# A two-layer hybrid decoder trunk: work at the chunks' ends moved by a few ticks, and the last pair of one mixer turned on TensorE

## The chip, the cores and the metric

The kernel runs on one core of a Trainium2 chip. The metric is the device time of one execution in microseconds (us), the median of the runs. All data is float32; every product of the projections is made of three matmuls of float32r parts.

## The reference

Two layers over 256 tokens of width 2048. Each layer is one RMS norm, one input projection, two mixers, a gate, and an output projection that is added to the residual stream; a last norm closes.

```python
def layer_even(x, norm_g, w_in, w_out):
    h = rmsnorm(x, norm_g)
    qa, ka, va, iq, ik, iw, qb, kb, vb, gate = split_cols(h @ w_in, SPLIT0)
    ...                      # rotary embedding on qa, ka, iq, ik, qb, kb
    o_a = dsa_attention(qa, ka, va, iq, ik, iw)   # 10 heads, one shared key/value head, 64 keys chosen per query
    o_b = dilated_attention(qb, kb, vb)           # 6 heads, three dilated windows, merged
    y = concatenate([o_a, o_b], axis=-1)
    return x + (y * silu(gate)) @ w_out

def layer_odd(x, norm_g, w_in, b_f, w_out):
    h = rmsnorm(x, norm_g)
    qc, kc, vc, qd, kd, vd, fl, gate = split_cols(h @ w_in, SPLIT1)
    o_c = stick_breaking_attention(qc, kc, vc)    # 8 heads; reverse cumulative sums of log(1 - sigmoid(z))
    log_f = log_sigmoid(fl + b_f)
    o_d = forgetting_attention(qd, kd, vd, log_f) # 8 heads; softmax with a running sum of log_f
    y = concatenate([o_c, o_d], axis=-1)
    return x + (y * silu(gate)) @ w_out
```

Each mixer's head makes scores of its queries and keys (causal), weights of the scores, and the weights times its values.

## The kernel before, in words

**Projections.** The columns of the two input and the two output projections are cut into 39 chunks ("jobs") of up to 512 columns, and TensorE does the jobs one after another; they are numbered from 0 (B5 is job 13, P0 job 14). Layer 0 has the jobs B0, K, I0, I1, B1, B2, B3, A0, A2, A4, A6, A8, B4, B5: a B job holds q, k, v and gate of one head, an A job q and gate of a pair of heads (A8 is the last pair, the heads 8 and 9), K and I are keys and indexer. P0 to P3 are the output projection. Layer 1 has C0, F1, G1, C2 to C7, D0 to D7, then Q0 to Q3. A job has 16 k-tiles of 128 input rows. For each k-tile and each half of the tokens, `products` (L323, L324, L326) issues hi times x-hi, hi times x-lo and lo times x-hi: six matmuls. One k-tile is a "tick".

**Weights.** SyncE loads them in pieces of four k-tiles, 1 MB (`load`, L256, tile raw, three buffers). For each half of a piece, `split` makes whi on ScalarE (L282, a rounding copy) and wlo on VectorE (L283, the rest). There are four buffers of each, so the splitting runs three halves ahead of TensorE. The first pieces are smaller, and x^T (tile xst) comes between them: `load_xT` (L626) sends the third and fourth k-tile from ScalarE's queue, the others from SyncE's.

**The work round of a head.** What a head needs beside its projection is written as a generator: it issues instructions, and `yield n` lets n ticks pass. After each k-tile `tick` advances all running generators, so their instructions land in each engine's queue between those of the splitting. Each engine, SyncE with its DMAs among them, works through its queue in the order in which it was issued. The round of a chunk begins when its projection ends, and runs beside the next two or three jobs on TensorE.

**Turning.** Queries, keys, weights of the attention and gates must be transposed. The "far" way is a 32x32 block transpose on VectorE into the tile far (`grid`, L428), a write to DRAM (`moved`, L437, tile fard) and a read-back (L448, or L442 where four reads keep the blocks in order). `gate_turned` does this for a gate at once, `gate_late` eight ticks later (L511). The "near" way is a transpose on TensorE (`turn`, L400, tile tp) and a cut from PSUM. Before, only B4, B5, D6 and D7 use it for their weights, and B5 and D7 for queries, keys and gate as well.

**The heads.** `heads_a` does a pair of A heads: rotary, gate u (L769), far turn of qk, scores and softmax of each head (`soft`, L549 and L551), weights (`share`, L565) turned far, cut into pAh/pAl and pBh/pBl (L477, L478), and six products into o (L464 to L466). For C and D, `vg1` makes v and the gate u by way of e = exp, a reciprocal on VectorE (L882) and two multiplications (L887); `stick` is the C head's weights (Exp, Ln and Relu on ScalarE, L939 to L942, a scan on VectorE, L945), `softmax_head` the D head's. The output products of all heads share one PSUM bank, o, and are multiplied by the turned gate uT (L532, L809).

Of the kernel before, what the change touches and what calls it, by code (L numbers as in the profile page):

```python
# [14 lines left out]
P = 128  # L15
# [159 lines left out]
def trunk(ctx, tc, x, xT, g1, w0, wo0, w1, wo1, bf, gf, consts, rope, out):  # L175
# [66 lines left out]
    def load():  # L242
        i = st["load"]
        if i == len(pieces):
            return
        st["load"] += 1
        wd, off, n, w = pieces[i]
        if i < len(FIRST):

            kt = sum(FIRST[:i])  # L250
            raws[i] = home[kt // 8][:, (kt % 8) * w:(kt % 8 + n) * w]
        else:
            raws[i] = wp.tile([P, n * w], F32, name="raw", tag="raw")
        if i == 1 or 3 < i < len(FIRST):
            load_xT(kt)
        nc.sync.dma_start(raws[i], wd[off:off + P * n * w].rearrange("(p f) -> p f", p=P))  # L256
        if i in (0, 2):
            load_xT(i)
        if i == len(FIRST) + 1:
            for th in range(NT):  # L260
                for c0, c1 in ((0, D),):
                    nc.sync.dma_start(xs[:, th, c0:c1], x[th * P:(th + 1) * P, c0:c1])
            nc.sync.dma_start(rt.rearrange("p a b -> p (a b)"), rope)
        if i == len(FIRST) + 2:
            nc.sync.dma_start(cons, consts)
# [235 lines left out]

    def gate_late(u, n=NT):

        box = []

        def way():
            yield 8
            t = grid([u])
            d = dr.tile([P, P * n], F32, name="fard", tag=f"fard{n}", bufs=4)
            yield 2  # L510
            nc.sync.dma_start(d, t)  # L511
            yield 4
            uT = hp.tile([P, P * n], F32, name="uT", tag="uT" if n == NT else "rl")
            read_back(uT, d, n)
            box.append(arrived(uT, n))

        start(way())
        return box
# [59 lines left out]

    def softmax_head(qk, ticks, nb, v, u, rs, kt, last, near):

        uT = u if last else gate_turned(u)
        qk = yield from qk_turned(qk, ticks, last)
        pr, l = soft(qk, nb() if callable(nb) else nb)
        if not last:
            yield 2
        share(pr, factor(l, rs))
        if near:
            yield 4
            blocks = quarters(turn([pr[:, 0:P], pr[:, P:SEQ], pr[:, SEQ:384]]))
        else:  # L590
            yield from moved(grid([pr]), pr, 2, 4, True)
            yield 4
            blocks = arrived(pr, 3)
        yield from weights_out(blocks, v, uT, kt, last)
# [14 lines left out]
    def load_xT(kt):  # L609
# [11 lines left out]
        for k in range(kt, kt + n):  # L621
            if k == kt or k == 9:
                m = min(kt + n, 9 if k < 9 else KT) - k
                t, j = (xst["a"], k - 1) if k < 9 else (xst["b"], k - 9)
                q = nc.scalar if k == 2 else nc.sync
                q.dma_start(t[:, j:j + m, :].rearrange("p a b -> p (a b)"), xT[:, KT + k * SEQ:KT + (k + m) * SEQ])  # L626

# [132 lines left out]
    def heads_a(ps, h):  # L760
# [3 lines left out]
        for th in range(NT):  # L764
            rotate(qk[:, th * 256:(th + 1) * 256], ps[th][:, 0:256], rt[:, th, 0:P], rt[:, th, 256:384], 2, P)
            tgs[1 - th] = hp.tile([P, 256], F32, name="tg", tag="tg")
            nc.scalar.activation(tgs[1 - th], ps[1 - th][:, 256:512], AF.Tanh, scale=hr0[:, 1 - th:2 - th])
        for th in (1, 0):
            nc.vector.scalar_tensor_tensor(u[:, :, th, :], tgs[th].rearrange("p (a b) -> p a b", a=2), 1.0,  # L769
                                           ps[th][:, 256:512].rearrange("p (a b) -> p a b", a=2),  # L770
                                           op0=OP.add, op1=OP.mult)
        uT = gate_late(u.rearrange("p a b c -> p (a b c)"), 4)
        yield from far([qk], qk, 2, 2, 4)
        yield 4
        q = arrived(qk, 4)
# [7 lines left out]
        js = [slice(j * P, (j + 1) * P) for j in range(2)]  # L783
        away = []
        for j in range(2):
            pr, l = soft((f[:, js[j]], kA, hi[:, js[j]], lo[:, js[j]], kAh, kAl), nbA)
            yield 2
            share(pr, factor(l, hr0))

            t = hp.tile([P, 512], F32, name="far", tag=("ih2", "il2")[j], bufs=1)[:, 0:384]  # L790
            start(moved(grid([pr], t), t, 2, 4, True))
            away.append(arrived(t, 3))
            yield 2
        yield 4

        ph, pl = (hp.tile([P, 2, SEQ], F32R, name="pA" + n, tag="i" + n, bufs=1) for n in "hl")
        p1h, p1l = (hp.tile([P, 2 * P], F32R, name="pB" + n, tag=t, bufs=1) for n, t in (("h", "y"), ("l", "sp")))
        for j in range(2):
            cut((quarters(ph[:, j, :]), quarters(pl[:, j, :])), away[j][:, 0:2])
            cut((quarters(p1h[:, js[j]]), quarters(p1l[:, js[j]])), away[j][:, 2:3])  # L800
            yield (8, 3)[j]
        uT, = uT
# [66 lines left out]

    def vg1(ps, o, apart=False, third=False):  # L870

# [3 lines left out]
        for th in range(NT):  # L875
            t = slice(th * P, (th + 1) * P)
            nc.scalar.activation(e[:, t], ps[th][:, o + P:o + 256], AF.Exp, scale=nr1[:, th:th + 1])  # L877
            upper(th)
        if apart:
            yield 1  # L880
        nc.vector.tensor_scalar(e, e, 1.0, 3.0e38, op0=OP.add, op1=OP.min)
        nc.vector.reciprocal(e, e)  # L882
        if apart:
            yield 1
        for th in range(NT):
            t = slice(th * P, (th + 1) * P)
            nc.vector.scalar_tensor_tensor(u[:, t], ps[th][:, o + P:o + 256], r1[:, th:th + 1], e[:, t],  # L887
                                           op0=OP.mult, op1=OP.mult)
        lower()
        return v, u  # L890
# [39 lines left out]
    def stick(qk, ticks, v, u, kt):  # L930

        uT = gate_late(u)
        qk = yield from qk_turned(qk, ticks, 0)
# [5 lines left out]
        nc.scalar.activation(sp, z, AF.Abs)  # L939
        nc.scalar.activation(sp, sp, AF.Exp, scale=-1.0)  # L940
        nc.scalar.activation(sp, sp, AF.Ln, bias=1.0)
        nc.scalar.activation(zp, z, AF.Relu)  # L942
        yield 6
        for _, s in BLK:
# [5 lines left out]
        yield from moved(grid([z]), z, 2, 4, True)  # L950
        yield 10
        yield from weights_out(arrived(z, 3), v, uT, kt, 0, 5)

    def head_c(ps, h):
        qk = scaled_qk(ps, 0, (0, 3), (1, 2))
        start(moved(grid([qk]), qk, 2, 4))
        v, u = yield from vg1(ps, 256, h == 0, h % 3 == 2)
        yield from stick(qk, 10 if h else 8, v, u, h)

    def head_cf(ps, qk):  # L960
        v, u = yield from vg1(ps, 0)
        yield from stick(qk, 10, v, u, 1)

    def head_d(ps, h):
        qk = scaled_qk(ps, 1, (0, 3), (1, 2))
        last = 2 * (h == HDD - 1)
        if not last:
            start(moved(grid([qk]), qk, 2, 4))
        v, u = yield from vg1(ps, 256, third=h == 0)
        yield from softmax_head(qk, 10, lambda: biases[h], v, u, None, HC + h, last, h >= HDD - 2)  # L970

# [125 lines left out]
```

## Time and profile before

| | |
|---|---|
| median of 3 runs | 898.07 us (895.04 to 900.7) |
| profiled execution | 896.82 us |
| its span, first to last instruction | 894.7 us |
| TensorE busy / its weight loads | 879.1 us (98%) / 734.5 us |
| VectorE, ScalarE, GpSimd busy | 659.0, 475.3, 50.2 us |
| DMA | 207.59 MB, 232 GB/s in the mean |
| chain that ended last | PE 79%, DVE 8%, DMA 6%, issue 3%, ACT 3% |

Matmuls overlap in the array: a row of the timeline gives start and duration, and the pace is read from one start to the next. A bracket such as [0.88 <-DVE wlo L283] is time for which the engine stood idle before this row, and what ended it. PE is TensorE, DVE VectorE, ACT ScalarE, SP SyncE, SPq its queue of DMA issues.

### The profile page before, as it was taken

The numbers are of one execution on the slowest core, as the hardware profiler recorded it, in microseconds if no ns is written. First come the engines' busy times: TensorE is split into PE (matmuls) and PEld (weight loads), VectorE is DVE, ScalarE is ACT, GpSimd is POOL, SyncE is SP. The second block draws the span as 40 slices with busy tenths as digits, with TensorE's granted clock in tenths as the row PEclk, the third lists the DMA queues.
The fourth block names the chain that finished last, engine by engine and source line by source line (L and its number), as shares of the span: only waits on it lengthen the run. The fifth ranks groups of instructions, "written<-read, shape, count | busy, mean of one in ns | idle before, by whom it ended". The sixth has DMA issues, their size and how long they took to land.

```text
span 894.7 us, 12055 instructions
## 1 busy us (share of the span) xinstructions
PE 879.1 (98%) x4185; PEld 734.5 (82%) x4185; DVE 659.0 (74%) x1162; ACT 475.3 (53%) x840; POOL 50.2 (6%) x69
## 2 busy tenths in 40 slices
PE   9999999999999999999999999999999999999996
PEld 6988888888888877888898888888777888888886
DVE  7587888877777777666667777777787777776563
ACT  7644555454454555555455555555555555555440
POOL 0013100000000000000000000000010000001110
PEclk9999999999999999999999999999999999999998
DMA  9887555676777765766486756666685776665542
GB/s 360 316 314 268 209 204 192 209 265 208 258 247 234 228 219 210 277 229 243 146 287 222 254 202 238 217 231 224 231 281 202 268 236 244 236 219 182 192 185 95
DMA packets 89661, 207.59 MB, mean 232 GB/s; under 512 B 32112, under 2 KB 60800, under 8 KB 71424
## 3 DMA queue, kind: packets, MB, share of 16 engines
q1 hardware_dynamic: 88128, 203.52, 64.7%
q0 software_dynamic: 896, 2.12, 0.8%
q10 hardware_dynamic: 576, 1.19, 0.4%
q8 instruction: 33, 0.54, 0.2%
q14 instruction: 28, 0.23, 0.1%
HBM read 185.29 MB, written 21.50 MB: 231 GB/s over the span
## 4 chain that ended last, share of the span: by engine, by line
PE 79%; DVE 8%; DMA 6%; issue 3%; ACT 3%; SPq 1%; POOL 0%; DVEq 0%; POOLq 0%; ACTq 0%
PE pj L323 25%; PE pj L324 25%; PE pj L326 25%; DVE wlo L283 3%; DMA raw<-in_w_out_dram 2%; DMA qk<-fard 2%; ACT whi L282 2%; DMA raw<-in_w_in_dram 1%; DMA fard<-far 1%; DVE far L428 1%; DVE e L882 1%; PE s L538 1%; PE o L531 0%; PE s L465 0%; PE s L466 0%
## 5 line engine op out<-in xcount | busy, mean ns | idle before, releaser
L283 DVE TENSOR_TENSOR wlo<-raw,whi 128x1024 fp32r<-128x1024 f32 (+3 forms) x300 | 352.6, 1189 | 149.7 <-ACT whi L282 148.2
L323 PE MATMUL pj<-whi,xh 128*128 128x512 f32 (+3 forms) x992 | 378.5, 383 | 0.0
L324 PE MATMUL pj<-whi,xl 128*128 128x512 f32 (+3 forms) x992 | 376.4, 381 | 0.0
L282 ACT ACTIVATE whi<-raw 128x1024 fp32r<-128x1024 f32 (+3 forms) x300 | 299.8, 1025 | 123.6 <-PE pj L324 73.4
L326 PE MATMUL pj<-wlo,xh 128*128 128x512 f32 (+3 forms) x992 | 297.3, 381 | 1.9 <-DVE wlo L283 1.8
L326 PEld LDWEIGHTS pj<-wlo,xh 128*128 128x128 f32 x992 | 182.9, 188 | 39.8 <-DVE wlo L283 4.5
L323 PEld LDWEIGHTS pj<-whi,xh 128*128 128x128 f32 x992 | 186.7, 188 | 34.0 <-ACT whi L282 1.3
L324 PEld LDWEIGHTS pj<-whi,xl 128*128 128x128 f32 x992 | 186.6, 188 | 33.0
L323 PE MATMUL pj<-whi,yh 128*128 128x512 f32 (+1 forms) x248 | 95.7, 386 | 0.0
L324 PE MATMUL pj<-whi,yl 128*128 128x512 f32 (+1 forms) x248 | 94.9, 383 | 0.0
L326 PE MATMUL pj<-wlo,yh 128*128 128x512 f32 (+1 forms) x248 | 76.7, 382 | 0.0
L326 PEld LDWEIGHTS pj<-wlo,yh 128*128 128x128 f32 x248 | 46.6, 188 | 9.2
L324 PEld LDWEIGHTS pj<-whi,yl 128*128 128x128 f32 x248 | 46.7, 188 | 8.7
L323 PEld LDWEIGHTS pj<-whi,yh 128*128 128x128 f32 x248 | 46.6, 188 | 8.6
L477 ACT ACTIVATE yh<-uT 128x256 fp32r<-128x256 f32 (+1 forms) x27 | 12.4, 458 | 61.1 <-DVE uT L532 45.2
L551 ACT ACTIVATE sn<-sn,nm 128x128 f32<-128x128 f32 (+1 forms) x48 | 21.5, 449 | 35.2 <-DVE nm L549 35.2
L598 ACT ACTIVATE sq<-xs 128x512 f32<-128x512 f32 x23 | 14.3, 623 | 30.2 <-DVE xs L821 26.5
L882 DVE RECIPROCAL e<-e 128x256 f32<-128x256 f32 x16 | 28.1, 1753 | 0.6
L382 POOL TENSOR_TENSOR qk<-rot,rot 128x256 f32<-128x256 f32 x16 | 11.9, 741 | 230.3 <-ACT sn L551 109.7
L948 ACT ACTIVATE z<-z 128x384 f32<-128x384 f32 x8 | 4.2, 526 | 38.0 <-DVE z L947 38.0
L877 ACT ACTIVATE e<-pj,nr 128x128 f32<-128x128 f32 x32 | 11.8, 367 | 21.9 <-DVE qk L867 21.9
L478 DVE TENSOR_TENSOR yl<-uT,yh 128x256 fp32r<-128x256 f32 (+1 forms) x27 | 12.8, 475 | 14.3 <-ACT yh L477 14.3
(216 smaller groups left out, 715.0 us busy)
## 6 DMA issues: line engine op xcount, KB each, us to landing
raw<-in_w_in_dram SPq DMA_DIRECT2D x108, 1024.0 KB, 6.1
raw<-in_w_out_dram SPq DMA_DIRECT2D x32, 1024.0 KB, 4.9
fard<-far SPq DMA_DIRECT2D x43, 256.0 KB, 2.1
qk<-fard SPq DMA_DIRECT2D x25, 256.0 KB, 5.2
fard<-far SPq DMA_DIRECT2D x28, 192.0 KB, 2.0
raw<-in_w_in_dram SPq DMA_DIRECT2D x4, 672.0 KB, 10.0
fard<-far SPq DMA_DIRECT2D x20, 128.0 KB, 4.6
uT<-fard SPq DMA_DIRECT2D x20, 128.0 KB, 4.2
```

Of the source, the lines that this page charges most:

```text
L282: nc.scalar.activation(hi, rw, AF.Copy)
L283: nc.vector.tensor_tensor(lo, rw, hi.bitcast(F32), op=OP.subtract)
L323: nc.tensor.matmul(o, a, wh, start=(kt == 0), stop=False)
L324: nc.tensor.matmul(o, b, wh, start=False, stop=False)
L326: nc.tensor.matmul(o, a, wl, start=False, stop=(kt == KT - 1))
L382: nc.gpsimd.tensor_tensor(dst, t1[:, 0:n], t2[:, 0:n], op=OP.add)
L477: nc.scalar.activation(dst[0], src, AF.Copy)
L478: nc.vector.tensor_tensor(dst[1], src, dst[0].bitcast(F32), op=OP.subtract)
L551: nc.scalar.activation(sn[:, s], sn[:, s], AF.Exp, scale=-1.0, bias=nm[:, th:th + 1], accum_out=l[:, th:th + 1])
L598: nc.scalar.activation(j, xs[:, th, c * 512:(c + 1) * 512], AF.Square, accum_out=ss[:, i, th, c:c + 1])
L877: nc.scalar.activation(e[:, t], ps[th][:, o + P:o + 256], AF.Exp, scale=nr1[:, th:th + 1])
L882: nc.vector.reciprocal(e, e)
```

## The change

It moves instructions of the work round by a few ticks and, for one pair of heads, replaces one way of turning by the other:

- A pairs: u is made four ticks later; the weights are written to DRAM after four ticks instead of two; the two heads' cuts are at new ticks (30 and 36, were 28 and 36) and the output products one k-tile later.
- The pair A8 turns its weights on TensorE: the scores of both heads stand two ticks apart, then three transposes and cuts for each head.
- C and D heads: v is finished first; e and the reciprocal come two ticks later, u two ticks after them. In `stick`, Ln and Relu come four ticks later, the scan two. The gate's turn is four ticks after u instead of eight, the same time as before.
- D heads use `gate_late` for their gate; D0 waits eight ticks instead of four for its turned weights.
- x^T's third and fourth k-tile come from SyncE's queue behind the second weights; x is loaded in four pieces instead of two.

```diff
@@ load, load_xT
-        if i == 1 or 3 < i < len(FIRST):
+        if i in (1, 2) or 3 < i < len(FIRST):
             load_xT(kt)
         nc.sync.dma_start(raws[i], ...)
-        if i in (0, 2):
-            load_xT(i)
+        if i == 0:
+            load_xT(0)
...
-                q = nc.scalar if k == 2 else nc.sync
-                q.dma_start(t[:, j:j + m, :]...)
+                nc.sync.dma_start(t[:, j:j + m, :]...)
@@ gate_late
-    def gate_late(u, n=NT):
+    def gate_late(u, first=8, n=NT):
...
-            yield 8
+            yield first
@@ softmax_head
-        uT = u if last else gate_turned(u)
+        uT = u if last else gate_late(u, 4) if rs is None else gate_turned(u)
...
-            yield 4
+            yield 8 if behind else 4
@@ heads_a
+        start(far([qk], qk, 2, 2, 4))
+        yield 4
         for th in (1, 0):
             nc.vector.scalar_tensor_tensor(u[:, :, th, :], ...)
-        uT = gate_late(u.rearrange("p a b c -> p (a b c)"), 4)
-        yield from far([qk], qk, 2, 2, 4)
-        yield 4
+        uT = gate_late(u.rearrange("p a b c -> p (a b c)"), 4, 4)
+        yield 8
...
+        near = h == HA - 2
+        scored = lambda j: soft((f[:, js[j]], kA, hi[:, js[j]], lo[:, js[j]], kAh, kAl), nbA)
...
+        def turned(j, pt):
+            cut((quarters(ph[:, j, :]), quarters(pl[:, j, :])), pt[:, 0:2])
+            cut((quarters(p1h[:, js[j]]), quarters(p1l[:, js[j]])), pt[:, 2:3])
+        if near:
+            sm = []
+            for j in range(2):
+                sm.append(scored(j))
+                yield 2
+                share(sm[j][0], factor(sm[j][1], hr0))
+            yield 1
+            ph, pl, p1h, p1l = rooms(("ih2", "il2"), ("ph", "pl"))
+            for j in range(2):
+                pr = sm[j][0]
+                turned(j, quarters(turn([pr[:, 0:P], pr[:, P:SEQ], pr[:, SEQ:384]])))
+                yield 3
+        else:
...
-            start(moved(grid([pr], t), t, 2, 4, True))
+                start(moved(grid([pr], t), t, 4, 4, True))
                 away.append(arrived(t, 3))
-            yield 2
-        yield 4
+                yield 2
+            yield 6
...
-        for j in range(2):
-            cut(...)
-            yield (8, 3)[j]
+            turned(0, away[0])
+            yield 6
+            turned(1, away[1])
+            yield 4
@@ vg1
-    def vg1(ps, o, apart=False, third=False):
+    def vg1(ps, o, apart=True, third=False):
...
+        lower()
         if apart:
-            yield 1
+            yield 2
         nc.vector.tensor_scalar(e, e, 1.0, 3.0e38, op0=OP.add, op1=OP.min)
         nc.vector.reciprocal(e, e)
         if apart:
-            yield 1
+            yield 2
...
-        lower()
@@ stick
-        uT = gate_late(u)
+        uT = gate_late(u, 4)
...
         nc.scalar.activation(sp, sp, AF.Exp, scale=-1.0)
+        yield 4
         nc.scalar.activation(sp, sp, AF.Ln, bias=1.0)
         nc.scalar.activation(zp, z, AF.Relu)
-        yield 6
+        yield 4
...
-        yield 10
+        yield 8
@@ head_c, head_cf, head_d
-        yield from stick(qk, 10 if h else 8, v, u, h)
+        yield from stick(qk, 6, v, u, h)
...
-        v, u = yield from vg1(ps, 256, third=h == 0)
-        yield from softmax_head(qk, 10, lambda: biases[h], v, u, None, HC + h, last, h >= HDD - 2)
+        v, u = yield from vg1(ps, 256, not last, h == 0)
+        yield from softmax_head(qk, 6, lambda: biases[h], v, u, None, HC + h, last, h >= HDD - 2, h == 0)
```

**SyncE, from one A pair's qk to the read-backs of its first head's weights.** raw is 1 MB of weights; fard is the DRAM buffer (128x512 for qk, 128x384 for one head's weights); far<-fard x4 are the four read-backs. Before:

```order
L437 DMA fard<-far 128x512
L256 DMA raw<-in_w_in_dram 128x2048
L437 DMA fard<-far 128x384
L448 DMA qk<-fard 128x4x128
L442 DMA far<-fard 32x4x96 x4
L256 DMA raw<-in_w_in_dram 128x2048
L437 DMA fard<-far 128x384
```

and in the change:

```order
L437 DMA fard<-far 128x512
L256 DMA raw<-in_w_in_dram 128x2048
L437 DMA fard<-far 128x384
L448 DMA qk<-fard 128x4x128
L256 DMA raw<-in_w_in_dram 128x2048
L442 DMA far<-fard 32x4x96 x4
L511 DMA fard<-far 128x512
L437 DMA fard<-far 128x384
```

A weight load now stands between the write of the first head's weights and its four read-backs; before, it stood behind them.

**VectorE, the end of the chunk C7.** pj are the projection's PSUM tiles, qk the scaled queries and keys, e the gate's denominator, u the gate, v the low part of the values, wlo a half of the coming weights. Before:

```order
L867 TENSOR_SCALAR qk<-pj_5679,rstd 128x128
L867 TENSOR_SCALAR qk<-pj_5680,rstd 128x128
L428 STREAM_TRANSPOSE far<-qk 128x4x4x32
L881 TENSOR_SCALAR e<-e 128x256
L882 RECIPROCAL e<-e 128x256
L887 SCALAR_TENSOR_TENSOR u<-pj_5679,rstd,e 128x128
L887 SCALAR_TENSOR_TENSOR u<-pj_5680,rstd,e 128x128
L490 SCALAR_TENSOR_TENSOR v<-pj_5679,rstd,v 128x128
L283 TENSOR_TENSOR wlo<-raw,whi 128x1024 x2
```

and in the change:

```order
L892 TENSOR_SCALAR qk<-pj_5667,rstd 128x128
L892 TENSOR_SCALAR qk<-pj_5668,rstd 128x128
L428 STREAM_TRANSPOSE far<-qk 128x4x4x32
L490 SCALAR_TENSOR_TENSOR v<-pj_5667,rstd,v 128x128
L283 TENSOR_TENSOR wlo<-raw,whi 128x1024
L907 TENSOR_SCALAR e<-e 128x256
L908 RECIPROCAL e<-e 128x256
L283 TENSOR_TENSOR wlo<-raw,whi 128x1024
L913 SCALAR_TENSOR_TENSOR u<-pj_5667,rstd,e 128x128
L913 SCALAR_TENSOR_TENSOR u<-pj_5668,rstd,e 128x128
L283 TENSOR_TENSOR wlo<-raw,whi 128x1024
```

Seven instructions besides the transpose stood ahead of two wlo in a row; now v is ahead of the first, e and its reciprocal stand behind it, and u behind the second.

**VectorE, the pair A8.** share is L565, the cuts pAl and pBl; uT is the gated output of a pair (L809 before, L834 in the change), yl its low part. Before, from the second head's share to the first head's cut:

```order
L565 TENSOR_SCALAR sn<-sn,sc 128x128
L565 TENSOR_SCALAR sn<-sn,sc 128x256
L428 STREAM_TRANSPOSE far<-sn 128x3x4x32
L283 TENSOR_TENSOR wlo<-raw,whi 128x1024
L809 TENSOR_TENSOR uT<-o,uT 128x4x4x32
L478 TENSOR_TENSOR yl<-uT,yh 128x512
L283 TENSOR_TENSOR wlo<-raw,whi 128x1024 x2
L478 TENSOR_TENSOR pAl<-far,pAh 128x256
L478 TENSOR_TENSOR pBl<-far,pBh 128x128
```

and in the change, from the same share to the second head's cut:

```order
L565 TENSOR_SCALAR sn<-sn,sc 128x128
L565 TENSOR_SCALAR sn<-sn,sc 128x256
L428 STREAM_TRANSPOSE far<-u 128x2x4x32
L283 TENSOR_TENSOR wlo<-raw,whi 128x1024
L478 TENSOR_TENSOR pAl<-tp,pAh 128x256
L478 TENSOR_TENSOR pBl<-tp,pBh 128x128
L283 TENSOR_TENSOR wlo<-raw,whi 128x1024
L834 TENSOR_TENSOR uT<-o,uT 128x4x4x32
L478 TENSOR_TENSOR yl<-uT,yh 128x512
L478 TENSOR_TENSOR pAl<-tp,pAh 128x256
L478 TENSOR_TENSOR pBl<-tp,pBh 128x128
L283 TENSOR_TENSOR wlo<-raw,whi 128x1024 x2
```

The block transpose (L428, far<-sn) is gone, the cuts read tp (a PSUM tile) instead of far, and the cut of the second head stands here instead of some ten instructions later.

## Rows read from the trace of the kernel before

**Rows 1.** The page, part 1: busy us (share of the span) x instructions.

```profile
PE 879.1 (98%) x4185; PEld 734.5 (82%) x4185; DVE 659.0 (74%) x1162; ACT 475.3 (53%) x840; POOL 50.2 (6%) x69
```

**Rows 2.** Waits of PE, whole span: us in total, times, longest us.

```profile
PE o L464 <- DVE uT L532: 1.8, 1, 1.8
PE pj L326 <- DVE wlo L283: 1.8, 4, 0.9
...
PE tp L912 <- DVE cq L909: 0.3, 1, 0.3
```

**Rows 3.** Timeline of PE, A pairs' output products: start us, us, instruction, idle before.

```profile
288.42 0.40 PE L464 MATMUL o<-pAh,vAh 128*128 128x512 f32 x1
289.31 0.50 PE L465 MATMUL o<-pAl,vAh 128*128 128x512 f32 x1 [0.49 <-DVE pAl L478]
...
313.38 0.50 PE L464 MATMUL o<-pAh,vAh 128*128 128x512 f32 x1
314.94 0.50 PE L465 MATMUL o<-pAl,vAh 128*128 128x512 f32 x1 [1.07 <-DVE pAl L478]
```

**Rows 4.** Timeline of PE, head B5's turns and scores.

```profile
334.48 0.44 PE L400 MATMUL tp<-cons,qk 128*128 128x128 f32 x2 [0.17 <-POOL qk L382]
335.63 0.44 PE L400 MATMUL tp<-cons,qk 128*128 128x128 f32 x2 [0.72 <-POOL qk L380]
...
339.46 0.49 PE L538 MATMUL s<-qkf 128*128 128x128 f32 x2 [0.30 <-ACT qkf L409]
...
340.57 0.39 PE L465 MATMUL s<-qkl,qkh 128*128 128x256 f32 x1 [0.50 <-DVE qkl L410]
```

**Rows 5.** Timeline of PE, transposes of B5's weights and gate.

```profile
348.20 0.49 PE L400 MATMUL tp<-cons,sn 128*128 128x128 f32 x3
348.53 0.38 PE L400 MATMUL tp<-cons,u 128*128 128x128 f32 x2
```

**Rows 6.** Timeline of PE, two chunk ends and D0's output products.

```profile
641.14 0.73 PE L326 MATMUL pj<-wlo,xh 128*128 128x512 f32 x2 [0.88 <-DVE wlo L283]
...
663.81 0.39 PE L323 MATMUL pj<-whi,xh 128*128 128x512 f32 x1
664.04 0.39 PE L324 MATMUL pj<-whi,xl 128*128 128x512 f32 x1
664.95 0.74 PE L326 MATMUL pj<-wlo,xh 128*128 128x512 f32 x2 [0.52 <-DVE wlo L283]
665.53 0.40 PE L323 MATMUL pj<-whi,xh 128*128 128x512 f32 x1
...
676.35 0.36 PE L464 MATMUL o<-ph,v 128*128 128x256 f32 x1 [1.82 <-DVE uT L532]
```

**Rows 7.** VectorE: its timeline at a chunk's end, then its waits, 550 to 670 us.

```profile
637.30 1.75 DVE L882 RECIPROCAL e<-e 128x256 f32<-128x256 f32 x1
...
639.87 2.35 DVE L283 TENSOR_TENSOR wlo<-raw,whi 128x1024 fp32r<-128x1024 f32 x2
...
DVE wlo L283 <- ACT whi L282: 24.0, 15, 3.1
```

**Rows 8.** 260 to 345 us: waits of SP and ACT, one transfer of the chain, far's landing.

```profile
SPq L442 <- DMA fard<-far: 29.6, 6, 5.6
...
ACT whi L282 <- DMA raw<-in_w_in_dram: 10.8, 5, 2.6
...
ACT whi L282 <- DMA raw<-in_w_out_dram: 3.5, 2, 1.8
...
288.68 8.05 DMA fard<-far
...
DMA to landing us min/median/max: 1.7/1.9/8.2
```

**Rows 9.** Busy us (x) of PE, PEld, DVE, ACT, POOL in job 13 (B5), then clock, DMA.

```profile
302.49:328.12 25.63, 24.53 (x113) 20.01 (x112) 19.21 (x42) 13.28 (x27) 1.48 (x2) 1.00 0.74 245
```

**Rows 10.** Timeline of ACT at the start.

```profile
6.25 0.63 ACT L282 ACTIVATE whi<-w0yh 128x512 fp32r<-128x512 f32 x1 [0.29 <-DMA w0yh<-in_w_in_dram]
```

More of the change, by code (lines that the diff above doesn't have):

```diff
@@ L253, in load @@
             raws[i] = wp.tile([P, n * w], F32, name="raw", tag="raw")
-        if i == 1 or 3 < i < len(FIRST):
+        if i in (1, 2) or 3 < i < len(FIRST):
             load_xT(kt)
         nc.sync.dma_start(raws[i], wd[off:off + P * n * w].rearrange("(p f) -> p f", p=P))
-        if i in (0, 2):
-            load_xT(i)
+        if i == 0:
+            load_xT(0)
         if i == len(FIRST) + 1:
             for th in range(NT):
-                for c0, c1 in ((0, D),):
+                for c0, c1 in ((0, 1024), (1024, D)):
                     nc.sync.dma_start(xs[:, th, c0:c1], x[th * P:(th + 1) * P, c0:c1])
@@ L577, in weights_out, with softmax_head @@
         weigh_out(ph, pl, p1, v, uT[0] if isinstance(uT, list) else uT, kt)
-    def softmax_head(qk, ticks, nb, v, u, rs, kt, last, near):
-        uT = u if last else gate_turned(u)
+    def softmax_head(qk, ticks, nb, v, u, rs, kt, last, near, behind=False):
+        uT = u if last else gate_late(u, 4) if rs is None else gate_turned(u)
         qk = yield from qk_turned(qk, ticks, last)
@@ L624, in load_xT @@
                 t, j = (xst["a"], k - 1) if k < 9 else (xst["b"], k - 9)
-                q = nc.scalar if k == 2 else nc.sync
-                q.dma_start(t[:, j:j + m, :].rearrange("p a b -> p (a b)"), xT[:, KT + k * SEQ:KT + (k + m) * SEQ])
+                nc.sync.dma_start(t[:, j:j + m, :].rearrange("p a b -> p (a b)"), xT[:, KT + k * SEQ:KT + (k + m) * SEQ])
     def feed0(kt, m):
@@ L783, in heads_a @@
         js = [slice(j * P, (j + 1) * P) for j in range(2)]
-        away = []
-        for j in range(2):
-            pr, l = soft((f[:, js[j]], kA, hi[:, js[j]], lo[:, js[j]], kAh, kAl), nbA)
-            yield 2
-            share(pr, factor(l, hr0))
-            t = hp.tile([P, 512], F32, name="far", tag=("ih2", "il2")[j], bufs=1)[:, 0:384]
-            start(moved(grid([pr], t), t, 2, 4, True))
-            away.append(arrived(t, 3))
-            yield 2
-        yield 4
-        ph, pl = (hp.tile([P, 2, SEQ], F32R, name="pA" + n, tag="i" + n, bufs=1) for n in "hl")
@@ L797, in heads_a, with rooms @@
[L797 to L800, printed above, removed]
-            yield (8, 3)[j]
+        near = h == HA - 2
+        scored = lambda j: soft((f[:, js[j]], kA, hi[:, js[j]], lo[:, js[j]], kAh, kAl), nbA)
+        def rooms(a, b):
+            return ([hp.tile([P, 2, SEQ], F32R, name="pA" + n, tag=t, bufs=1) for n, t in zip("hl", a)]
+                    + [hp.tile([P, 2 * P], F32R, name="pB" + n, tag=t, bufs=1) for n, t in zip("hl", b)])
@@ new lines, in turned @@
+        def turned(j, pt):
[14 more added lines that the diff above has]
+        else:
+            away = []
+            for j in range(2):
+                pr, l = scored(j)
+                yield 2
+                share(pr, factor(l, hr0))
+                t = hp.tile([P, 512], F32, name="far", tag=("ih2", "il2")[j], bufs=1)[:, 0:384]
+                start(moved(grid([pr], t), t, 4, 4, True))
+                away.append(arrived(t, 3))
+                yield 2
+            yield 6
+            ph, pl, p1h, p1l = rooms(("ih", "il"), ("y", "sp"))
+            turned(0, away[0])
+            yield 6
+            turned(1, away[1])
+            yield 4
@@ L883, in vg1 @@
         if apart:
-            yield 1
+            yield 2
         for th in range(NT):
@@ L956, in head_c @@
         start(moved(grid([qk]), qk, 2, 4))
-        v, u = yield from vg1(ps, 256, h == 0, h % 3 == 2)
-        yield from stick(qk, 10 if h else 8, v, u, h)
+        v, u = yield from vg1(ps, 256, True, h % 3 == 2)
+        yield from stick(qk, 6, v, u, h)
     def head_cf(ps, qk):
         v, u = yield from vg1(ps, 0)
-        yield from stick(qk, 10, v, u, 1)
+        yield from stick(qk, 6, v, u, 1)
     def head_d(ps, h):
```

## The prediction, made before the change was run

> **What bounds the kernel now.** I read the page's busy line first [rows 1]: TensorE is busy for 98% of the span, so time can only come from the places where TensorE stands still, or from work taken off it. The second view is the list of what TensorE waited for [rows 2]. It is short: one output product that waits 1.8 us for the previous head's uT on VectorE, four waits of 1.8 us together for a wlo, one for cq. The third view is TensorE's timeline at these places and at those of the A pairs and of head B5. There the start-to-start distance tells more than the bracket: in the steady row of [rows 6], 663.81 to 664.04, a projection matmul follows the last after 0.23 us, and 664.04 to 664.95 is 0.91, so 0.68 were lost where the bracket says 0.52. The fourth view says why VectorE was late: its timeline at a chunk's end [rows 7] and, for layer 0, SyncE's and ScalarE's waits [rows 8].
>
> **Part by part.**
>
> *A pairs.* SyncE issues in order. Before, it stood 29.6 us in six waits for a write to DRAM to land before it could issue the four read-backs, and the next 1 MB of weights stood behind them; ScalarE then waited 10.8 us in five waits for weights, and the cuts of the turned probabilities came late [rows 8]. On TensorE that is an o product at 289.31 (0.89 behind the one before it, so 0.66 lost) and one at 314.94 (1.56, so 1.33 lost) [rows 3]. The change puts one weight load ahead of each group of read-backs, moves u's two VectorE instructions four ticks back and the output products one k-tile later (a k-tile is 6 times 0.23, 1.4 us). Gain 2.0; bounds 0 and 2.0.
>
> *B5's start.* Head B5 turns on TensorE directly behind this, and stops four times: 0.17, 0.72, 0.30 and 0.50, 1.7 in all [rows 4]. Ahead of them stand the same late weights: ScalarE waited 3.5 us more, in two waits, for the output projection's first loads [rows 8], and qk's cuts are queued behind on ScalarE. With the weights issued ahead, and with the last pair's output products gone from this stretch, I take 1.7; bounds 0 (POOL, which makes qk, is not touched) and 1.7.
>
> *The last A pair on TensorE.* Two writes and eight read-backs leave SyncE's queue, and two grid transposes leave VectorE; six transposes come to TensorE. The rows for such transposes are [rows 5]: three start at 348.20, the next two at 348.53, so 0.11 each, 6 x 0.11 = 0.65 lost. All of it is on the path, because TensorE is the bound. [...]
>
> The pair's second scores now come after two k-tiles and not four, and its outputs in job 13 and not 14, so what VectorE and ScalarE do for it stands closer. In that job VectorE is busy for 19.21 of 25.63 us [rows 9]; it loses the two grid transposes and takes over one cut and one output step. TensorE can now wait for the scores' PSUM bank, for the share ahead of the transposes, or for the cut ahead of the output products. No row shows these waits; the nearest are the waits for a cut, 0.49 and 1.07 [rows 3]. Nothing from below (if VectorE keeps its lead), three waits of 1.07, 3.2, from above. I take 0.6, near one of the smaller kind, because the cut now reads PSUM and no DMA stands in the way.
>
> *Chunk ends of layer 1.* After a head's projections, VectorE did qk, a grid transpose, e, the reciprocal (1.75 us), u twice and v in one block, and only at 639.87 the two wlo [rows 7]; TensorE got the first of them at 641.14 after 0.88 idle, and at the next head at 664.95 [rows 6]. Now v comes first, then a wlo, then e and the reciprocal, then a wlo, then u; and Ln and Relu leave the block on ScalarE. The block ahead of the first wlo is thus shorter by most of the 2.6 us between 637.30 and 639.87, and the largest stall is 0.9: it should go. The listed four waits are 1.8; each shows 0.16 too little (0.68 for 0.52), and the second wlo comes another 0.1 late (664.95 to 665.53, two matmuls, is 0.58 for 0.46): 1.8 + 4 x 0.27 = 2.9. Bounds 0 (the wlo waits for ScalarE's whi and not for VectorE's turn) and 2.9. I take 2.9. The same order frees cq's copy: 0.3, from [rows 2]. What is late next is ScalarE's whi, with Ln and Relu moved behind it; VectorE's earlier wlo then has only that to wait for.
>
> *D0.* The first D head's output product waits 1.82 for the last C head's uT: with the 0.16 that a bracket shows too little, 2.0 lost [rows 6]. The change lets D0 come four ticks later, 5.4 us, behind that uT. Gain 2.0; bounds 1.5 and 2.0, since the wait it leaves is longer than the delay only if uT is late by more than 7 us.
>
> *Start.* Two k-tiles of x^T go from ScalarE's queue to SyncE's behind the second weights. ScalarE waited 0.29 for those weights at 6.25 [rows 10], and cuts this x^T right behind. The weights may land up to 0.3 sooner; the x^T, now behind them, may come late by as much. I take 0, and keep 0.3 either way. The finer load of the residual stream, four pieces for two, is for work that is needed late: 0.
>
> **The sum.** Gains 2.0 + 1.7 + 2.9 + 0.3 + 2.0 = 8.9; costs 0.65 + 0.6 = 1.25; net 7.65. The profiled execution took 896.82 us (span 894.7 and 2.1 around it), so 889.2; the median of the three runs is 1.25 above it, so 890.4. One per cent, about what a measurement of this kernel can tell from no change, is 9.0 us: 889.1 is the line.
>
> **The rivals.**
> (a) *All of it and no new wait*: net 8.9 - 0.65 = 8.25, and up to 1.5 more, a guess, from stalls too small to be listed: 888.3 to 889.8. For it: the list of TensorE's waits holds nothing else of size. Against: job 13 is fuller. Chance 0.17.
> (b) *Half comes back in jobs 13 and 14*: VectorE, in order, becomes the wait there: the bound of 3.2 in place of 0.6, and B5's 1.7 stays. Net 7.65 - 2.6 - 1.7 = 3.35: 894.7. For it: 19.21 of 25.63 busy is the densest row I have. Against: VectorE's own waits there are for ScalarE, which gets its weights earlier. Chance 0.17.
> (c) *The chunk ends do not move*: VectorE's wlo waited 24.0 us in 15 times for ScalarE's whi between 550 and 670 us [rows 7]. If that, and not the block, is what TensorE feels, 2.9 stays: net 4.75, 893.3; the change then does not do what its words say. Against: the first late wlo started straight behind v, with no wait of its own. Chance 0.10.
> (d) *Slower: read-backs behind the weights.* In four pairs the read-backs now stand behind a 1 MB load. A write behind such a load took 8.05 us to land, a read-back alone 1.9 [rows 8]: 6.2 later. Two ticks (2.7) of slack are given, so the o products could wait 3.5 in each of four pairs, 14 in all; less the other gains, 6.9, plus 1.25, is +8.35: 906.4. It decides from a landing 6.0 us after issue: there 1.4 per pair eats the rest. Against: the load is issued while SyncE would have waited for the write, so part of it is over when the read-backs come. Beside this stands the Trainium skill, "DMA: Bandwidth & Descriptors", "Queues, rings and completion order": SyncE owns one ring per DMA engine, whose descriptors are consumed in order. By that rule the read-backs do wait for the whole load; the 8.05 row agrees. Chance 0.06.
>
> **Numbers.** The forecast has 0.50, with its own range 888.5 to 892; it comes to 890.4. The range is 886 to 896: from all gains with the start's 0.3 and the runs' spread below, to (b) and (c) with the spread above; it leaves out (d) and the tails. Faster by over 1%: two thirds of (a), 0.11, and a good third of the forecast, 0.19: 0.30. Slower by over 1%: (d), 0.06. The rest, 0.64, is within 1%.
>
> **What would show it.** In the changed profile the rows of [rows 2] should be gone: no o that waits for uT at D0, no wlo at the chunk ends. ScalarE's waits for weights in layer 0 should fall well below 10.8, and SyncE's for the write should cost no weights. Six more transposes stand at 0.11 each. TensorE's waits in job 13 tell between the forecast, (a) and (b); far's landing times in the A stretch tell whether (d) holds. The prediction is wrong if new waits on TensorE sum to more than 3 us, or if the chunk ends keep theirs.

## The result, and the profile after

The changed kernel took 889.1 us in the median of five runs (888.21 to 889.44) against 898.07; the ratio is 0.9901 with a 95% interval of 0.9871 to 0.9930. That is 9.0 us, the line between "within 1%" and "faster by over 1%" that the prediction drew; it forecast 890.4, range 886 to 896. The profiled execution took 889.15 us, its span is 887.3.

The page and TensorE's list of waits, over the whole span (us in total, times, longest us):

```profile
PE 877.5 (99%) x4191; PEld 735.9 (83%) x4191; DVE 656.4 (74%) x1160; ACT 474.7 (53%) x840; POOL 51.0 (6%) x69
...
PE s L1040 <- DVE mhalf L1036: 1.2, 1, 1.2
PE tp L937 <- DVE cq L934: 0.4, 1, 0.4
```

Every wait of [rows 2] but the one for cq is gone; the first row is the warm-up at the start and stands in the kernel before too. On TensorE's timeline, the output products of the two A pairs of [rows 3], B5's transposes of [rows 4] and D0's products of [rows 6] now read:

```profile
290.67 0.39 PE L464 MATMUL o<-pAh,vAh 128*128 128x512 f32 x1
290.90 0.39 PE L465 MATMUL o<-pAl,vAh 128*128 128x512 f32 x1
...
315.97 0.28 PE L466 MATMUL o<-pBh,vAl 128*128 128x256 f32 x1
316.09 0.49 PE L400 MATMUL tp<-cons,sn 128*128 128x128 f32 x3
316.33 0.48 PE L323 MATMUL pj<-whi,xh 128*128 128x512 f32 x1
316.65 0.40 PE L324 MATMUL pj<-whi,xl 128*128 128x512 f32 x1
...
334.44 0.60 PE L400 MATMUL tp<-cons,qk 128*128 128x128 f32 x4
...
673.84 0.61 PE L326 MATMUL pj<-wlo,xh 128*128 128x512 f32 x2
674.29 0.28 PE L464 MATMUL o<-ph,v 128*128 128x256 f32 x1
```

No row has a bracket. 290.67 to 290.90 is the plain pace, 0.23, where [rows 3] had 0.89 and 1.56. B5's four transposes are one row instead of two with 0.17 and 0.72 ahead of them. Three new transposes (316.09) take 0.24 to the next matmul's start, and that one's successor is 0.32 behind it instead of 0.23: 0.33 for a group, 0.66 for the six.

A row without a bracket is not always on time. The two places of [rows 6] where a wlo was late now read:

```profile
634.98 0.39 PE L324 MATMUL pj<-whi,xl 128*128 128x512 f32 x1
635.21 0.62 PE L326 MATMUL pj<-wlo,xh 128*128 128x512 f32 x2
...
658.08 0.40 PE L324 MATMUL pj<-whi,xl 128*128 128x512 f32 x1
658.54 0.73 PE L326 MATMUL pj<-wlo,xh 128*128 128x512 f32 x2
```

The first, in job 28, keeps the plain pace. The second, in job 29, still starts 0.46 behind the matmul ahead of it, though the list of waits does not name it.

Where the time went can be read without any bracket: both kernels do the same 3792 projection matmuls, so the start of a job's first one, before and after, shows how far the changed kernel is ahead.

| first projection matmul of | before, us | after, us | after minus before | this stretch |
|---|---|---|---|---|
| job 1 | 27.69 | 28.70 | +1.01 | start: +1.01 |
| job 11 | 254.30 | 255.19 | +0.89 | -0.12 |
| job 15 | 357.56 | 353.97 | -3.59 | A pairs, B5: -4.48 |
| job 25 | 560.73 | 557.22 | -3.51 | cq's stretch: +0.08 |
| job 29 | 655.20 | 649.12 | -6.09 | chunk ends: -2.58 |
| job 31 | 704.66 | 696.51 | -8.15 | a last chunk end, D0: -2.06 |
| last one of all | 887.35 | 879.18 | -8.17 | -0.02 |
| end of the span | 894.71 | 887.33 | -7.38 | last store: +0.79 |

The last row is no work of the change. From the last projection matmul on, the engines' instructions stand at the same distances in both traces. The last store is issued 3.4 us behind that matmul in both, and lands 6.46 behind it before and 7.24 after. In the runs below the rest takes between 7.3 and 8.2 us, whatever the kernel (7.35 with the gate in one block, 8.18 with Ln and Relu put back).

For layer 0 the waits of SyncE and ScalarE between 260 and 345 us, and the landing times of the read-backs alone (L442, from 255 us on), answer to [rows 8]:

```profile
SPq L442 <- DMA fard<-far: 3.6, 2, 2.5
...
ACT pAh L477 <- DMA far<-fard: 1.1, 1, 1.1
...
DMA to landing us min/median/max: 2.8/4.2/6.2
```

SyncE stands 3.6 us where it stood 29.6; ScalarE's waits for weights, 14.3 in the two rows before, are no longer in the list. The read-backs do land later behind a weight load: 4.2 us after their issue in the median, where it was 1.9 and at most 2.3 before (the 8.2 in [rows 8] is a write to DRAM, which that row counts together with the read-backs). The ticks cover it but for ScalarE's 1.1. The start is the place that got worse; ScalarE's timeline there:

```profile
5.06 0.63 ACT L282 ACTIVATE whi<-w0yh 128x512 fp32r<-128x512 f32 x1
7.51 0.51 ACT L635 ACTIVATE xh<-xst,x 128x256 fp32r<-128x256 f32 x1 [1.82 <-DMA xst<-in_xT_dram]
```

The second weights do come earlier (5.06 for 6.25 in [rows 10]), but x^T's third k-tile is now waited for 1.82 us.

### The profile page after: what moved, and what is told of

Read it like the earlier page. It is cut to its first block, busy times and chain, and to the rows that moved or that the text cites. A ratio compares the mean times of both kernels' runs of the same rounds, so it can differ in the third digit from the quotient of the medians.

```text
span 887.3 us, 12056 instructions
## 1 busy us (share of the span) xinstructions
PE 877.5 (99%) x4191; PEld 735.9 (83%) x4191; DVE 656.4 (74%) x1160; ACT 474.7 (53%) x840; POOL 51.0 (6%) x69
## 4 chain that ended last, share of the span: by engine, by line
PE 92%; DVE 2%; issue 2%; DMA 2%; ACT 1%; POOL 0%; POOLq 0%; DVEq 0%; ACTq 0%
PE pj L323 29%; PE pj L326 29%; PE pj L324 29%; DVE wlo L283 1%; PE s L538 1%; DMA w0yh<-in_w_in_dram 1%; ACT whi L282 1%; PE o L531 1%; PE s L465 1%; DMA raw<-in_w_in_dram 1%; PE s L464 1%; PE s L466 1%; PE o L464 0%; PE o L465 0%; PE o L466 0%
## 5 line engine op out<-in xcount | busy, mean ns | idle before, releaser
L599 ACT ACTIVATE sq<-xs 128x512 f32<-128x512 f32 x23 | 14.3, 623 | 28.4 <-DVE xs L846 27.1
```

What stands on the lines that cost most here:

```text
L599: nc.scalar.activation(j, xs[:, th, c * 512:(c + 1) * 512], AF.Square, accum_out=ss[:, i, th, c:c + 1])
```

## The experiments

Each kernel differs from the one named by the edit shown or, where it is long, told in words. A time is the median of its runs; "ahead" is counted at the projection matmuls as in the table.

**x^T back on ScalarE's queue.** The change, with

```diff
-        if i in (1, 2) or 3 < i < len(FIRST):
+        if i == 1 or 3 < i < len(FIRST):
...
-        if i == 0:
-            load_xT(0)
+        if i in (0, 2):
+            load_xT(i)
...
-                nc.sync.dma_start(t[:, j:j + m, :]...)
+                q = nc.scalar if k == 2 else nc.sync
+                q.dma_start(t[:, j:j + m, :]...)
```

> The changed kernel with the third and fourth k-tile of x^T back on ScalarE's queue; all else as in the change. Theory (the move costs the start): in the changed trace ScalarE waits 1.82 us for this x^T, and the 60th projection matmul stands 1.01 us later than before; with the move undone that comes back, 889.1 - 1.0 = 888.1, and the 60th matmul starts near 12.7 us after the first instruction. Rival (the start is set by the order of all loads, or by x in four pieces, not by this transfer): 889.1, and the 60th matmul near 13.7.

888.51 us (888.11 to 889.07), and job 1 starts at 27.89 instead of 28.70. One execution is not enough here, because the start varies; but all fourteen traces of this study can be used, eight with the old order of x^T and six with the new one. The matmul 60 places into job 0 starts, old order: 19.53, 19.59, 19.65, 19.73, 19.80, 19.97, 20.00, 20.65, mean 19.87; new: 20.25, 20.50, 20.53, 20.54, 20.65, 20.75, mean 20.54. The move costs 0.7 us in the mean, and 1.0 between the two profiled runs that the prediction was about. One start with the old order is as late as the new ones (20.65, the A pairs alone); there ScalarE waited 2.21 us for the second weights.

**The last A pair over DRAM.** The change, with

```diff
-        near = h == HA - 2
+        near = False
```

> The changed kernel with the last A pair turned over DRAM like the other pairs. Theory (the order on SyncE's queue is what cured the A pairs, turning the last pair on TensorE only costs its transposes): the six transposes go, 889.1 - 0.55 = 888.6, and no new wait in jobs 12 to 14. Rival (it is the last pair's DRAM traffic and its work in job 14 that made B5's turns late): TensorE waits again in job 14, 1.5 to 3 us, 890.5 to 892.

888.26 us (887.55 to 889.03); jobs 11 to 14 are 5.18 shorter than before, where the change has 4.48, and TensorE waits for nothing there. So turning the pair on TensorE cost 0.70, the price of its six transposes, and cured nothing; the rival falls.

**The A pairs alone; C and D alone.** The kernel before with one half of the change each (for C and D alone, `gate_late` keeps its eight ticks for the A pairs).

> The kernel before with the change to the A pairs alone (order on SyncE's queue, later cuts, last pair on TensorE). Theory (the parts add): jobs 11 to 14 get shorter by 4.5 us and nothing else moves, 896.8 - 4.5 = 892.3; the chunk ends of layer 1 keep their waits for wlo (1.8 us) and D0 its wait for uT (1.8). Rival (layer 1's late wlo come from loads that lag since layer 0): layer 1's waits shrink too, under 891.

> The kernel before with the change to the C and D heads alone (order in the gate and the weights, D0 later, gate turned later). Theory (the parts add): layer 0 keeps its stops (pAl 1.6 us, B5's four 1.7 us), layer 1 gets shorter by 4.5 us, 896.8 - 4.5 = 892.3. Rival (VectorE's order is not what made wlo late, the loads are): the waits for wlo stay, only D0's 2.0 go, 894.8.

891.73 us (891.32 to 892.28) and 892.22 us (890.97 to 893.42). With the A pairs alone jobs 11 to 14 shrink by 4.48, and TensorE's waits of layer 1 stay, the one for uT at 1.1 instead of 1.8:

```profile
PE pj L326 <- DVE wlo L283: 1.8, 4, 0.9
...
PE o L464 <- DVE uT L532: 1.1, 1, 1.1
```

With C and D alone the waits for pAl (1.4), qk, qkf and qkl (1.9 together) stay, and jobs 25 to 30 shrink by 4.55. By these stretches the halves add. D0's wait for uT varies by itself: 1.8 and 2.0 in two kernels with the old tick, 1.1 in four others.

**Which part of the A pairs' edit.** The order on SyncE's queue alone (the kernel before, with the one number changed that the cut shows), and the later u, cuts and output products without that order and with the last pair over DRAM as before:

```diff
-            start(moved(grid([pr], t), t, 2, 4, True))
+            start(moved(grid([pr], t), t, 4, 4, True))
```

> The kernel before with one number changed: the A pairs' weights are written to DRAM four ticks after their block transpose instead of two, which puts a weight load ahead of each group of read-backs on SyncE's queue; u, cuts and output products stay where they were. Theory (the late weights behind SyncE's wait are the cause, but the cuts need the two ticks): ScalarE's waits for weights between 260 and 345 us fall from 14.3 to under 3, B5's four stops (1.7) go, the A pairs' output products still wait for their cuts, 1.5 to 3: 895 to 896. Rival (the cuts have room): the whole 5 us of the A part come, 892.

> The kernel before with u four ticks later and the A pairs' cuts and output products later as in the change, but the order on SyncE's queue as before, and the last pair over DRAM. Theory (SyncE's order is the cause): ScalarE still waits over 10 us for weights, the output products no longer wait for a cut (1.6 gone), B5's stops (1.7) stay: 895. Rival (the later products alone are the cure): all stops of jobs 11 to 14 go, 892.

Neither gains anything: 897.32 us (895.1 to 899.99, ratio 1.0005, 0.9990 to 1.0019) and 897.48 (894.26 to 901.48, ratio 1.0004, 0.9987 to 1.0020). With the order alone the waits for weights are gone, but ScalarE now stands before a cut; its waits, and its timeline before the last pair's scores:

```profile
ACT pAh L477 <- DMA far<-fard: 10.3, 3, 3.5
```

```profile
303.02 0.42 ACT L477 ACTIVATE pAh<-far 128x256 fp32r<-128x256 f32 x1 [3.38 <-DMA far<-fard]
303.34 0.29 ACT L477 ACTIVATE pBh<-far 128x128 fp32r<-128x128 f32 x1
303.54 0.40 ACT L779 ACTIVATE qqh<-qk 128x256 fp32r<-128x256 f32 x1
```

The next pair's qqh is queued behind that cut, and TensorE's scores wait for what comes behind it: 1.5 in three times for qqf and 0.9 for B5's qkf; from start to start the three largest cost 3.0. This is what the two ticks are for. With the later cuts alone, SyncE stands 27.9 and ScalarE waits 13.2 and 1.7 for weights, about as before, and B5's first transposes come still later, with an effect on TensorE's clock that the last section shows. Of what was expected, the weights' side came in both: ScalarE's waits for them go with the order and stay without it. TensorE's side did not come as said. With the order alone the output products no longer wait for their cuts, the scores wait in their place, and B5 keeps part of its stops; with the later cuts alone 0.7 of the waits for pAl is left. The times, 895 to 896 and 895, were too good by about 2.

**Which part of the C and D edit.** The gate's e, reciprocal, u and v in one block again, and Ln and Relu directly behind Exp again, each in the changed kernel:

```diff
-    def vg1(ps, o, apart=True, third=False):
+    def vg1(ps, o, apart=False, third=False):
...
-        lower()
         if apart:
-            yield 2
+            yield 1
...
+        lower()
...
-        yield from stick(qk, 6, v, u, h)
+        yield from stick(qk, 10 if h else 8, v, u, h)
```

```diff
         nc.scalar.activation(sp, sp, AF.Exp, scale=-1.0)
-        yield 4
         nc.scalar.activation(sp, sp, AF.Ln, bias=1.0)
         nc.scalar.activation(zp, z, AF.Relu)
-        yield 4
+        yield 8
```

> The changed kernel with the gate's e, reciprocal, u and v of the C and D heads in one block again as before (all later ticks as in the change; Ln and Relu stay moved). Theory (that block makes the wlo at the chunk ends late): TensorE waits for wlo four or five times again, 2.9 to 3.2 us, 892.1. Rival (Ln and Relu on ScalarE, or loads, were the cause): under 0.5 us comes back, 889.3.

> The changed kernel with Ln and Relu of the C heads directly behind Exp again, everything else at its changed tick. Theory (VectorE's block alone decides): no new wait, 889.1. Rival (ScalarE's two activations, some 1 us ahead of a whi at the chunk end, matter as much): the waits at the chunk ends come back in part, 1 to 2 us, 890.5.

Both theories fall. With the block back: 887.67 us (886.84 to 888.75), no wait for a wlo in TensorE's list, and jobs 25 to 30 are 5.48 shorter than before, 0.84 more than in the change. With Ln and Relu back: 896.41 (895.36 to 897.6), nearly all of the gain lost, jobs 25 to 30 even 1.79 longer than before. TensorE's list names no wlo there either: the loss is in matmuls that start 0.34 to 0.46 apart instead of 0.23, and in scores that wait for qkl. Another 1.9 is lost in jobs 15 to 24, most of it in job 21; the run with the block back loses 1.1 there in its trace too, so that part comes and goes. So the block on VectorE, on which the prediction rested, was not what made wlo late.

What did so is seen at a C chunk's end (first matmul of job 27) if both engines are read side by side. The kernel before, ScalarE and then VectorE:

```profile
607.34 0.53 ACT L939 ACTIVATE sp<-z 128x384 f32<-128x384 f32 x1 [1.76 <-DVE z L936]
607.89 0.53 ACT L940 ACTIVATE sp<-sp 128x384 f32<-128x384 f32 x1
608.45 0.53 ACT L941 ACTIVATE sp<-sp 128x384 f32<-128x384 f32 x1
608.88 0.51 ACT L942 ACTIVATE zp<-z 128x384 f32<-128x384 f32 x1
609.30 1.04 ACT L282 ACTIVATE whi<-raw 128x1024 fp32r<-128x1024 f32 x1
...
611.89 0.37 ACT L877 ACTIVATE e<-pj,nr 128x128 f32<-128x128 f32 x1 [1.04 <-DVE qk L867]
```

```profile
606.75 0.55 DVE L936 TENSOR_TENSOR z<-s,cons 128x384 f32<-128x384 f32 x1
610.37 1.23 DVE L283 TENSOR_TENSOR wlo<-raw,whi 128x1024 fp32r<-128x1024 f32 x1 [3.07 <-ACT whi L282]
611.51 0.60 DVE L867 TENSOR_SCALAR qk<-pj,rstd 128x128 f32<-128x128 f32 x2
```

The engines wait for each other in turn: ScalarE for z, VectorE 3.07 us for the whi behind ScalarE's four activations, ScalarE for qk behind that wlo. Ln (608.45) and Relu (608.88) stand in this chain: from Exp's start at 607.89 to that whi it is 1.41 us, and their results are used only ticks later, by the scan. With them put back into the changed kernel, VectorE has that wait and another one, because v no longer has the block behind it to bridge the time until the next whi:

```profile
612.01 1.23 DVE L283 TENSOR_TENSOR wlo<-raw,whi 128x1024 fp32r<-128x1024 f32 x1 [3.07 <-ACT whi L282]
613.16 0.60 DVE L892 TENSOR_SCALAR qk<-pj,rstd 128x128 f32<-128x128 f32 x2
613.79 0.71 DVE L428 STREAM_TRANSPOSE far<-qk 128x512 f32<-128x512 f32 x1
614.43 0.31 DVE L490 SCALAR_TENSOR_TENSOR v<-pj,rstd,v 128x128 fp32r<-128x128 f32 x1
615.66 1.23 DVE L283 TENSOR_TENSOR wlo<-raw,whi 128x1024 fp32r<-128x1024 f32 x1 [0.92 <-ACT whi L282]
```

The theory formed from this was tried by itself: the kernel before, with Ln and Relu moved and nothing else.

```diff
         nc.scalar.activation(sp, sp, AF.Exp, scale=-1.0)
+        yield 4
         nc.scalar.activation(sp, sp, AF.Ln, bias=1.0)
         nc.scalar.activation(zp, z, AF.Relu)
-        yield 6
+        yield 4
...
-        yield 10
+        yield 8
```

> The kernel before with Ln and Relu of the C heads four ticks later (the scan two ticks later) and nothing else. Theory formed from the runs with the gate or with Ln and Relu put back (the two activations stand in a chain from z over whi and wlo to the next chunk's qk and e): VectorE's longest wait for whi at a C chunk's end falls from 3.1 to 2.1, the waits for wlo at the chunk ends go, 3.2 us; D0's wait for uT stays, 894. Rival (both halves of the C and D part are needed, as with the A pairs): the waits for wlo stay, 896.8.

892.93 us (891.18 to 893.17, ratio 0.9944, 0.9924 to 0.9964). TensorE waits for no wlo any more, and at the same chunk's end the whi starts 0.43 behind Exp's start instead of 1.41, and VectorE waits 0.97 less. ScalarE, then VectorE:

```profile
605.86 0.52 ACT L940 ACTIVATE sp<-sp 128x384 f32<-128x384 f32 x1
606.29 1.04 ACT L282 ACTIVATE whi<-raw 128x1024 fp32r<-128x1024 f32 x1
```

```profile
604.71 0.56 DVE L936 TENSOR_TENSOR z<-s,cons 128x384 f32<-128x384 f32 x1 [0.36 <-PE s L466]
607.37 1.23 DVE L283 TENSOR_TENSOR wlo<-raw,whi 128x1024 fp32r<-128x1024 f32 x1 [2.10 <-ACT whi L282]
```

Jobs 25 to 30 are 4.19 shorter, of the change's 4.64; 0.75 of that is D0's wait for uT, which is 1.1 here and in runs that touch nothing in C and D. Jobs 25 to 28, where no D0 product stands, tell it most plainly: 2.58 shorter with Ln and Relu moved alone, 2.5 to 2.6 with the gate in pieces as well (the change, in two traces), 3.85 longer with the gate in pieces and Ln and Relu put back.

**D0 without its extra ticks.** The change, with

```diff
-        ... h >= HDD - 2, h == 0)
+        ... h >= HDD - 2)
```

> The changed kernel with D0's four extra ticks taken out. Theory (D0's products have to come behind the last C head's uT): TensorE waits for uT at D0 again, 1 to 2 us, 890.5. Rival (uT is no longer late, since Ln and Relu left the chunk's end): no wait, 889.1.

890.16 us (890.0 to 890.75): TensorE waits 1.1 for uT again, and jobs 25 to 30 lose 1.3 to 1.4 against the two traces of the change. The four ticks pay.

**The parts that paid.** The change with three parts taken out: x^T's move, the last pair on TensorE, the gate in pieces.

> The parts that paid, put together: the change without its move of x^T, with the last A pair over DRAM, and with the gate of the C and D heads in one block as before; Ln and Relu, D0, the order on SyncE's queue and the later cuts as in the change. Theory (the three taken out cost 0.9, 0.6 and nothing or more): 889.1 - 0.9 - 0.6 = 887.6, up to 1.4 less if the block order itself is worth what its run alone showed, 886.2. Rival (the parts hide each other, as the A pair's two halves did): 889 or more.

> The changed kernel once more, beside the chosen version on the same chip: 889.1 if nothing differs between chips; TensorE's 60th projection matmul starts at 20.5, as in the other runs with x^T behind the second weights.

886.21 us (885.42 to 886.4), ratio 0.9870 (0.9851 to 0.9890) to the kernel before; the change on the same chip 888.74 (888.38 to 889.48), 0.9902 (0.9887 to 0.9918). The version with fewer edits is 2.5 us faster than the change. At the last projection matmul it is 10.68 ahead of the kernel before, the change 8.17 and 8.96. One wait is left beside the warm-up's:

```profile
PE pj L323 <- ACT whi L282: 0.8, 1, 0.8
```

## Why the prediction was right, and where it failed

The sum, net 7.65, was made against a profiled execution of 896.82 and gave 889.2; the changed one took 889.15. That is closer than its terms deserve: the A pairs and B5 gave 2.0 more than forecast, the start and the last store took 1.8 of it back, and that these meet is luck. The 1.25 added for the median did not come: the changed kernel's median is 889.1, its profiled execution 889.15.

Term by term:

- **A pairs, B5 and the last pair** were 3.7 gained and 1.25 lost, net 2.45; measured 4.48. The six transposes cost 0.66 to 0.70 for the 0.65 taken from [rows 5]. The Trainium skill ("TensorE: Matmul & The Clock Gate", Part 4, on the PE-mode transpose) measured about 275 ns for one in a kernel's context, 1.65 us for six by estimate. The trace agrees on the duration, 270 to 273 ns each, but the next one starts after 0.11 us, and that distance is what a busy TensorE pays. The new waits in job 13, taken at 0.6, are not there at all: none is listed for TensorE between 240 and 345 us, and from start to start none shows either. The stops were worth 5.1 to 5.2, not 3.7: 2.4 at the A pairs for the 2.0, and 2.8 at B5 for the 1.7. I added brackets for B5, and a bracket leaves out what its successors lose.
- **The chunk ends** failed as a step: "shorter by most of the 2.6 us between 637.30 and 639.87, and the largest stall is 0.9: it should go". The size nearly came out, 2.6 for jobs 25 to 28 against 2.9, but the end in job 29, the 664.95 of [rows 6], brought nothing, and the block is not the cause: in one piece again it costs nothing and even pays 0.8. The cause is rival (c)'s ScalarE, with the two activations that the change moves as well; (c) priced it as no gain, because it left out that move. The row that said so was there, VectorE's 24.0 us of waiting for whi in [rows 7]; I argued it away because the late wlo itself had no bracket. It had none because VectorE had waited earlier in the same chain.
- **D0**: 2.0 forecast, 2.04 measured behind the twelfth k-tile of job 29. The ticks alone are worth 1.3 to 1.4: the wait of 1.82 was a long one, and kernels with the old tick that waited 1.1 have the other 0.74 without it.
- **Start**: taken as 0 with 0.3 either way; +1.01 in the profiled run, +0.7 in the mean of all traces. The bound was wrong: the weights came 1.2 sooner, not 0.3, and x^T still cost more. I bounded the loss by the gain, and looked at when x^T is needed but not at what lies ahead of it in SyncE's queue.
- **cq**: 0.3 forecast, 0.08 lost in the first trace of the change, 0.5 gained in the second (no wait for cq there). It comes and goes.

Of the rivals, (a), no new wait, is what happened in layer 0; the median, 889.1, lies in its range too, but the start's cost was no part of it. (b) did not come: jobs 13 and 14 show no wait. (d) did not come either: the read-backs landed 2.3 later in the median and 4.3 at most, not 6.2, because they were issued 1.6 to 2.9 us after the load ahead of them, which took 5.3 to 7.6 to land. By the rule of the Trainium skill named there ("DMA: Bandwidth & Descriptors", "Queues, rings and completion order") they queue behind it, and the trace agrees: two of the loads landed at 273.27 and 298.50, the first read-backs behind them at 273.47 and 298.69. But a rule on order says nothing of how much of the load is left. One read-back landed 6.2 after its issue, past the 6.0 at which (d) was to decide, and TensorE waited for nothing. The order alone shows where (d) would begin: without the two ticks of slack, ScalarE waits 10.3 us for them.

Not settled: why the gate in one block is 0.84 better than in pieces. All of it lies at one chunk's end, in the first twelve k-tiles of job 29: 0.86 gained with the block, 0.02 with the pieces, where the matmul at 658.54 is still late. VectorE's second wait, 0.92 for a whi, is not enough to explain it: the change has it at each chunk's end, and in jobs 25 to 28 it costs nothing.

## What to carry to other kernels

When two engines wait for each other in turn, the late instruction need not have a bracket of its own: follow the chain back over both engines until an instruction stands in it that nobody waits for yet, and move that one. Count gains from start to start of the work that both kernels share, not from brackets. And take each part of an edit out again once: here three of the parts cost 2.5 us together, and one pair of parts was worth nothing until both were there.

## What the hardware showed that was not expected

In the run with the later cuts alone, TensorE stood 1.44 and 0.72 us at B5's first transposes, and then its projection matmuls started 0.43 apart instead of 0.23, from 336.72 to 340.06. The stretches of that trace (busy us and count of PE, PEld, DVE, ACT, POOL, then granted clock, DMA share, GB/s) and its rows:

```profile
333.00:336.50 3.50, 1.34 (x8) 0.68 (x7) 2.90 (x10) 2.79 (x9) 1.45 (x2) 1.00 0.83 287
336.50:338.50 2.00, 2.00 (x7) 1.57 (x6) 1.34 (x5) 1.04 (x2) 0.00 (x0) 0.57 1.06 446
338.50:340.50 2.00, 2.00 (x7) 1.57 (x6) 1.95 (x4) 2.00 (x6) 0.00 (x0) 0.57 1.01 344
340.50:344.00 3.50, 3.50 (x21) 2.97 (x20) 2.72 (x10) 2.23 (x8) 0.00 (x0) 1.00 0.75 222
```

```profile
334.82 0.44 PE L400 MATMUL tp<-cons,qk 128*128 128x128 f32 x2 [1.44 <-POOL qk L382]
335.98 0.44 PE L400 MATMUL tp<-cons,qk 128*128 128x128 f32 x2 [0.72 <-POOL qk L380]
...
338.78 0.63 PE L324 MATMUL pj<-whi,yl 128*128 128x512 f32 x1
339.21 0.63 PE L323 MATMUL pj<-whi,yh 128*128 128x512 f32 x1
```

The granted clock was at the lower of its two levels, 1.2 GHz, for most of the second and third stretch, right behind the two stops; eight matmuls took 3.34 us instead of 1.84, so 1.5 were lost beside the stops themselves. In the kernel before, the stops at the same place sum to 1.7, and its clock stays at 1.00 there in the profiled execution; but its runs spread over 894.65 to 900.7 us, those of the changed kernel over 888.21 to 889.48. The mean granted clock of each execution goes with it. Of 43 executions of the kernel before, eight have 0.994 to 0.996 and took 899.3 us in the mean, the other 35 have 0.997 to 0.999 and took 897.0; no execution of the changed kernel is below 0.997. So some executions of the kernel before lose the clock for a while, and take some 2 us longer. That it happens at B5's stops, as in the trace above, is likely but not shown: no trace of such an execution was kept.
